# A recurrence step's small matmuls put in one fixed order in TensorE's queue, and its preparation moved to ordinary rank

## The chip, the core and the metric

One core of one Trainium2 chip runs the whole kernel. The metric is the time of one execution on the device in microseconds (us). The kernel before took 2898.03 us, the median of three runs (2893.39, 2898.03 and 2906.78 us).

## The reference, cut to what matters

One layer of a hybrid backbone works on 1024 latent tokens and 256 context tokens, all in float32. A joint input projection feeds two groups of heads. The first is differential attention, 8 heads over 1792 keys. The second is an RWKV-7 recurrence with 16 heads of size 64 that is scanned in both directions; one step of it is

```
sa = einsum('bhvk,bhk->bhv', S, -kk_t)
S  = S * w_t[:, :, None, :] + sa[..., None] * b_t[:, :, None, :] + v_t[..., None] * k_t[:, :, None, :]
y  = einsum('bhvk,bhk->bhv', S, r_t)
```

The gated outputs of both groups go through one output projection, a residual add and a final norm. The kernel doesn't scan token by token: it takes 32 tokens (a chunk) at once, so that a step of the recurrence becomes a few small matrix products.

## The kernel before, in words

**The stages.** The kernel first normalizes the tokens and makes the modulation. Then comes the long stage of input projections (lines 336 to 338), which also prepares, for each pair of heads, the recurrence's operands: the line-451 products with their mask, the transposes of line 455, and spills to DRAM. The third stage, `mix_phase`, holds the recurrence, the attention, the norm of the recurrence's outputs and the output projection. A tail finishes the attention's last blocks and the last part of the projection.

**The recurrence.** Heads are taken in two sets of eight (four pairs of heads, in two duos). A set has five segments of 256 tokens, first the context's and then four of the latents; a segment has eight chunks. That makes 80 steps, one for each chunk. Two steps in a row are a *part* (40 parts): the operands of a part are loaded together into one of two slots (tiles `L` and `R`, `load_part`, lines 774 to 784), and the inverses that its chunks need are loaded into one tile `Tb` (`load_inv`, line 795). All loads are issued on SP's queue.

**A step**, function `step`, in the order of its text:

- The *corrections*: 16 matmuls (line 907), each with a 96-row, 32-column stationary operand and 64 moving columns, in four column positions of the array (0, 32, 64, 96), into the left half of PSUM tile `bank[0]`. Four ScalarE copies (line 914) bring them into `R`. If the step is the last of its part, the first half of the next part's *preparation* follows (`prep(j + 1, 0, yb)`): 16 matmuls with 32 by 32 stationary operands (line 805) and four ScalarE copies into `L` (line 808).
- `fill(0)`: a share of the other work is emitted here: attention blocks by a running credit, the inverses, norms, and the projection.
- The *state group*: 16 matmuls (line 926) with 128-row, 64-column stationary operands in two column positions (0, 64), into `bank[1]`; then four VectorE multiplies by the decay (line 937), which write the next step's state into `R`.
- The *output group*: 16 matmuls (line 950), 128 rows by 32 columns, in four column positions, into the right half of `bank[0]`, and one ScalarE copy (line 952). In the last step of a part, the second half of the preparation (`prep(j + 1, 1, yb)`) follows.
- `fill(1)`: the rest of the step's share of other work.

Every float32 matmul stands in the trace as two passes, so a group of 16 matmuls counts x32. Both preparation halves use the one PSUM tile `yb`. The state group of part j + 1 reads what both halves wrote; its corrections read the loaded part of `L` alone.

**What sets the order.** Each engine works its queue in order. The queue's order is made at build time: a scheduler takes, among the instructions that it holds to be ready, the one with the lowest rank; the rank is the place in the text. `ahead(500)` (a high-priority block) ranks what stands in it 500 places earlier, and on leaving the block the count goes on from where it stood when the block was entered. So the state group's block and the output group's block, which follow one another, begin at the same rank. All three groups and both halves of the preparation stand in such blocks. `held(x)` makes the first matmul of a group wait, by semaphore, for all four copies or multiplies that came before it; the other fifteen have only the waits of their own operands.

Of the kernel before, what the change touches and what calls it, by code (L numbers as in the profile page):

```python
# [83 lines left out]
def tile_kernel(ctx: ExitStack, tc: tile.TileContext, i: dict, o: dict, heads=H, phases=3):  # L84
# [38 lines left out]
    with ExitStack() as p1:  # L123
# [373 lines left out]
        def b_k(p):  # L497
# [43 lines left out]
            if p == heads - 1:  # L541
                yield
                yield from b_inv()
                if phases >= 2:
                    pr.close()
                    mix.append(mix_phase(p2, tc, i, o, s, ident, nhalf, dram, td0, neglam, subg, lnh, heads, psm))
                    yield from mix[0]
# [195 lines left out]
def mix_phase(ctx, tc, i, o, s, ident, nhalf, dram, td0, neglam, subg, lnh, heads, psm):  # L743
    nc = tc.nc
# [7 lines left out]
    for w in duos:  # L752
        for n in range(2):
            L = cp.tile([P, 2, 2, 2, HN, P], F32, name=f"L{w}{n}")
            R = cp.tile([P, HN, 2, 2, P], F32, name=f"R{w}{n}")
# [42 lines left out]
    def prep(j, w, pp):  # L798
        L = slots[w, j % 2][0]
        Tb = Tbs[j][:, 2 * w:2 * w + 2]  # L800
        for e in range(2):
            for c in range(HN):
                for q in range(4):
                    n = 96 * (HN * e + c)
                    nc.tensor.matmul(pp[32 * q:32 * q + 32, n:n + 96], Tb[96:128, e, HN * q + c, :],  # L805
                                     L[96:128, e, q // 2, q % 2, c, 0:96], start=True, stop=True, tile_position=(96, 32 * q))
        for q in range(4):
            nc.scalar.copy(L[96:128, :, q // 2, q % 2, :, 0:96],  # L808
                           pp[32 * q:32 * q + 32, 0:192 * HN].rearrange("p (e c y) -> p e c y", e=2, y=96))
# [28 lines left out]
    bank = [psx.tile([P, 512], F32, name=f"bank{n}") for n in range(2)]  # L838
    yb = psx.tile([P, 512], F32, name="yb")
# [41 lines left out]
    def ahead(n):  # L881
        return tc.high_priority(offset=n) if n else nullcontext()
# [3 lines left out]
    def hold(x):  # L886
        whole.append(x.ins.name)

    def held(x):
        for y in whole:  # L890
            tc.add_manual_dep(x.ins, y, mybir.DependencyInfo(mybir.DependencyClass.Sync, mybir.DependencyReason.DATA))
        whole.clear()

    def step(j, k, fill):
        m, f = j // NF, j % NF
        c = HN * f + k
        p0, sg = items[m]
        hv = lambda h: slice(64 * h, 64 * h + 64)
        later_prep = k == HN - 1 and j + 1 < n_part
        with ahead(HPC):  # L900
            for d in range(2):
                for e in range(2):
                    for w in duos:
                        L, R = slots[w, j % 2]
                        for h in range(2):
                            u, o_ = 64 * w + 32 * h, 128 * d + 64 * e
                            x = nc.tensor.matmul(bank[0][u:u + 32, o_:o_ + 64], L[0:96, e, h, d, k, 96:128],  # L907
                                                 R[0:96, k, d, e, hv(h)], start=True, stop=True, tile_position=(0, u))
                            held(x)
            for w in duos:  # L910
                R = slots[w, j % 2][1]
                for h in range(2):
                    u = 64 * w + 32 * h
                    hold(nc.scalar.copy(R[96:128, k, :, :, hv(h)],  # L914
                                        bank[0][u:u + 32, 0:256].rearrange("p (d e v) -> p d e v", d=2, e=2)))
            if later_prep:
                prep(j + 1, 0, yb)
        fill(0)
        with ahead(HPC):
            for w in duos:  # L920
                L, R = slots[w, j % 2]
                for e in range(2):
                    for d in range(2):
                        for h in range(2):
                            o_ = 256 * w + 128 * d + 64 * e
                            x = nc.tensor.matmul(bank[1][hv(h), o_:o_ + 64], L[:, e, h, d, k, 0:64],  # L926
                                                 R[:, k, d, e, hv(h)], start=True, stop=True, tile_position=(0, 64 * h))
                            held(x)
            for w in duos:
                if k < HN - 1:  # L930
                    dst = slots[w, j % 2][1][0:64, k + 1]
                elif f == NF - 1 and sg == 3:
                    continue
                else:
                    dst = slots[w, (j + 1) % 2][1][0:64, 0]
                for h in range(2):
                    hold(nc.vector.tensor_tensor(dst[:, :, :, hv(h)], bank[1][hv(h), 256 * w:256 * w + 256].rearrange("p (d e v) -> p d e v", e=2, d=2),  # L937
                                                 wcs[p0][hv(h), 2 * w:2 * w + 2, sg + 1, :, c:c + 1].rearrange("p e d o -> p d e o").broadcast_to([HD, 2, 2, HD]), op=ALU.mult))
        g = c // HN
        if k == 0:  # L940
            ysb[m, g] = cp.tile([P, HN, NL, HD], F32, tag="ys", name=f"ys{m}_{g}", bufs=YBUF)
        with ahead(HPY):
            for w in duos:
                L, R = slots[w, j % 2]
                for e in range(2):
                    o_ = 256 + P * w + 64 * e
                    for h in range(2):
                        for d in range(2):
                            q = 64 * d + 32 * h
                            nc.tensor.matmul(bank[0][q:q + 32, o_:o_ + 64], L[:, e, h, d, k, 64:96], R[:, k, d, e, hv(h)],  # L950
                                             start=True, stop=True, tile_position=(0, q))
            nc.scalar.copy(ysb[m, g][:, k], bank[0][:, 256:512].rearrange("p (x v) -> p x v", x=NL))  # L952
            if later_prep:
                prep(j + 1, 1, yb)
        fill(1)

    def store_y(m, g):
        p0, sg = items[m]
        y = ysb.pop((m, g))
        for d in range(2):  # L960
            t0 = tok0(sg, d)
            for h in range(2):
                q = 64 * d + 32 * h
                dst = s["y"][p0 // NL, t0:t0 + SEG, d, h].rearrange("(c t) w v -> t c (w v)", t=CH)
                dst = (dst[:, ::-1] if d else dst)[:, HN * g:HN * g + HN]
                nc.sync.dma_start(dst, y[q:q + 32].rearrange("t c x v -> t c (x v)"))
# [449 lines left out]
    def turn(q, k=0):  # L1416
        if len(q) > k and next(q[k], "end") == "end":
            q.pop(k)
# [10 lines left out]
    def fill(pos):  # L1429
        for _ in range(2):  # L1430
            state["credit"] += total / (4 * n_tick) * RATES[2 * state["t"] // n_tick]
            while state["credit"] > 0 and state["n"] < heads * NT - NT + 6:
                r = next(att, None)
                if r is None:
                    break
                turn(outs)
                state["credit"] -= r
            while state["ninv"] < 33 * (state["t"] + INVA + _ / 4 + pos / 2) / NC:
                next(state["inv"], None)
                state["ninv"] += 1  # L1440
            turn(norms)
            turn(norms, 1)
            turn(projs)
# [8 lines left out]
    for t in range(n_tick):  # L1452
        m, c = t // NC, t % NC
        p0, sg = items[m]
        j, k = t // HN, t % HN
        state["t"] = t
        for f in later.pop(t, []):
            f()
        if c == 0:
            for w in duos:  # L1460
                start_item(w, m)
            if sg == 2 and m + 2 < n_item:
                load_pairs(m + 2)
        if 1 <= j and j + 1 < n_part:
            if k == 0:
                load_part(j + 1)
        step(j, k, fill)
        if k == HN - 1:
            at(t + 1, lambda m=m, g=c // HN: store_y(m, g))
        if c < NC - 1:  # L1470
            continue
        for sg_, gs in ((-1, (8,)), (2, (2, 4)), (3, (0, 6))):
            if sg == sg_:
                for g0 in gs:
                    for w in duos:
                        at(t + 3, lambda p=p0 + 2 * w, g0=g0: norms.append(norm(p, g0)))
        if sg == (3 if m < 5 else 0):
            for w in duos:
                at(t + 1, lambda j=p0 // 2 + w: projs.append(project(j)))
# [97 lines left out]
```

## Time and profile before

| | us |
|---|---|
| median of three runs | 2898.03 |
| profiled execution, its own time | 2893.28 |
| its span, first to last instruction | 2891.3 |
| TensorE busy in the span | 2751.5 |
| VectorE busy | 1477.8 |
| ScalarE busy | 1224.6 |
| GpSimd busy | 1130.1 |

The profile's engines are PE (TensorE's matmuls), PEld (its weight loads, beside PE), DVE (VectorE), ACT (ScalarE), POOL (GpSimd) and SP (SyncE, which only issues DMAs here). Idle time of an engine counts only where the others wait for it. The recurrence's loop stands between 1242 us (its first correction starts at 1242.61 us) and 2612 us (its last state product starts at 2610.89 us); what comes before is the projections' stage, and what comes after is the tail.

### The profile page before, as it was taken

How to read it: one execution, taken by the hardware profiler on the slowest of the kernel's cores; microseconds unless marked ns; L12 is line 12 of the kernel's file. 1: busy time of each engine (PE TensorE's matmuls, PEld its weight loads, DVE VectorE, ACT ScalarE, POOL GpSimd, SP SyncE). 2: the span in 40 equal slices, each digit the busy share in tenths (PEclk: the TensorE clock that was granted, in tenths of full speed). 3: DMA queues.
4: the chain of work that ended last, by engine and by line, in shares of the span. 5: the costliest groups of instructions: out<-in, count | busy, mean ns of one | idle time of the engine just before them, and what ended most of it. 6: DMA issues, size and time to landing. Idle time of an engine off the chain costs nothing.

```text
span 2891.3 us, 60416 instructions
## 1 busy us (share of the span) xinstructions
PE 2751.5 (95%) x23907; PEld 2156.8 (75%) x23907; DVE 1477.8 (51%) x2950; ACT 1224.6 (42%) x2528; POOL 1130.1 (39%) x1665
## 2 busy tenths in 40 slices
PE   6999999999999999889999999999999999998886
PEld 5888888888788887767667767776777777776675
DVE  5655656464555554324544445454643343445667
ACT  3333434333333433224545445554544454444343
POOL 4243432434333334733552533561662110105365
PEclk9999999999999999968999989999999999999898
DMA  7466655566556556695676655747566578548534
GB/s 232 102 156 165 172 150 152 153 168 155 140 141 158 145 154 157 159 209 125 138 147 121 140 111 109 155 89 177 134 148 172 139 169 175 138 108 234 169 124 164
DMA packets 518010, 437.55 MB, mean 151 GB/s; under 512 B 157831, under 2 KB 462131, under 8 KB 512608
## 3 DMA queue, kind: packets, MB, share of 16 engines
q1 hardware_dynamic: 515632, 427.94, 59.3%
q0 software_dynamic: 2096, 5.75, 1.1%
q8 instruction: 189, 3.10, 0.5%
q14 instruction: 93, 0.76, 0.1%
HBM read 258.69 MB, written 163.86 MB: 146 GB/s over the span
## 4 chain that ended last, share of the span: by engine, by line
PE 75%; DMA 7%; DVE 6%; POOL 5%; SPq 3%; ACT 3%; issue 2%; POOLq 0%; DVEq 0%; ACTq 0%
PE bank L926 12%; PE bank L950 10%; PE sc L1069 6%; PE po L1114 5%; PE pa L1099 3%; PE pg L451 3%; PE yb L805 2%; PE pso L1322 2%; PE pso L1324 2%; PE pso L1323 2%; PE bank L907 1%; PE ptk L455 1%; PE psg_v L338 1%; PE psg_v L336 1%; PE psg_v L337 1%
## 5 line engine op out<-in xcount | busy, mean ns | idle before, releaser
L926 PE MATMUL bank<-R,L 128*64 128x64 f32 x2560 | 429.3, 250 | 6.7 <-ACT R L914 5.9
L950 PE MATMUL bank<-R,L 128*32 128x64 f32 x2560 | 390.0, 235 | 0.0
L926 PEld LDWEIGHTS bank<-R,L 128*64 128x64 f32 x2560 | 250.2, 138 | 146.5 <-issue 20.8
L937 DVE TENSOR_TENSOR R<-bank,wc 64x256 f32<-64x256 f32 x312 | 131.5, 421 | 432.1 <-PE bank L926 419.5
L1069 PE MATMUL sc<-ka,q 128*128 128x512 f32 (+1 forms) x832 | 285.4, 435 | 18.9 <-DVE pb L1072 18.0
L1072 DVE TENSOR_SCALAR_CACHE_REDUCE pb<-sc,mn 128x512 f32<-128x512 f32 x256 | 191.5, 748 | 142.3 <-PE sc L1069 135.0
L1077 ACT ACTIVATE pb<-pb,mn 128x1536 f32<-128x1536 f32 (+1 forms) x160 | 218.2, 1364 | 80.3 <-DVE pb L1072 76.3
L950 PEld LDWEIGHTS bank<-R,L 128*32 128x32 f32 x2560 | 178.4, 109 | 92.8 <-issue 4.3
L952 ACT COPY ys<-bank 128x256 f32<-128x256 f32 x80 | 29.8, 372 | 464.6 <-PE bank L950 444.0
L1114 PE MATMUL po<-vk,aT 128*128 128x128 f32 x1600 | 223.4, 282 | 1.0 <-ACT aT L1101 1.0
L1114 PEld LDWEIGHTS po<-vk,aT 128*128 128x128 f32 x1600 | 206.2, 195 | 15.4 <-ACT aT L1101 1.8
L736 POOL TENSOR_TENSOR tmp<-aw,tt 128x31 f32<-128x31 f32 (+15 forms) x310 | 163.4, 527 | 126.2 <-DMA y<-ys 35.5
L481 POOL TENSOR_SCALAR ta<-ta,ka 128x256 f32<-128x256 f32 x80 | 85.6, 1070 | 294.1 <-DVE bk L479 293.9
L458 ACT COPY km<-ptk 64x256 f32<-64x256 f32 x320 | 117.4, 367 | 188.3 <-PE ptk L455 160.4
L738 POOL TENSOR_TENSOR tt<-tt,tmp 128x31 f32<-128x31 f32 (+15 forms) x310 | 181.1, 584 | 20.3
L1069 PEld LDWEIGHTS sc<-ka,q 128*128 128x128 f32 x832 | 136.9, 195 | 53.5 <-DVE pb L1072 30.4
L1091 DVE SCALAR_TENSOR_TENSOR pb<-pb,cc,pb 128x512 f32<-128x512 f32 (+1 forms) x208 | 165.2, 841 | 2.0
L808 ACT COPY L<-yb 32x384 f32<-32x384 f32 x312 | 146.3, 469 | 33.5 <-PE yb L805 29.1
L1101 ACT COPY aT<-pa 128x512 f32<-128x512 f32 (+1 forms) x208 | 115.1, 569 | 80.7 <-PE pa L1099 78.5
L452 DVE TENSOR_TENSOR km<-pg,msk 128x512 f32<-128x512 f32 x80 | 55.1, 688 | 179.7 <-PE pg L451 159.1
L1306 POOL TENSOR_TENSOR olo<-of,ohi 128x512 fp32r<-128x512 f32 x30 | 38.9, 1296 | 266.5 <-ACT ohi L1305 216.3
L1072 DVE TENSOR_SCALAR_CACHE_REDUCE pb<-sc 128x512 f32<-128x512 f32 (+1 forms) x160 | 101.2, 635 | 81.2 <-PE sc L1069 76.5
(354 smaller groups left out, 6555.2 us busy)
## 6 DMA issues: line engine op xcount, KB each, us to landing
kt<-km SPq DMA_DIRECT2D x160, 256.0 KB
L<-kt SPq DMA_DIRECT2D x80, 512.0 KB
acc<-acc SPq DMA_DIRECT2D x50, 512.0 KB
ra<-ra SPq DMA_DIRECT2D x160, 128.0 KB
L<-ra SPq DMA_DIRECT2D x80, 256.0 KB
R<-vb SPq DMA_DIRECT2D x160, 64.0 KB
y<-ys SPq DMA_DIRECT2D x160, 64.0 KB
yn<-y SPq DMA_DIRECT2D x40, 256.0 KB
```

The source lines that it names most:

```text
L458: nc.scalar.copy(km[64 * h:64 * h + 64, e:NC:2, 0:HD], pt[64 * e:64 * e + 64, :, 64 * h:64 * h + 64])
L736: e.tensor_tensor(mv, aw[:n, t, t + 1:CH].unsqueeze(2).broadcast_to([n, w, j]), tt[:n, t:t + 1, 0:j].broadcast_to([n, w, j]), op=ALU.mult)
L738: e.tensor_tensor(tt[:n, t + 1:CH, 0:j], tt[:n, t + 1:CH, 0:j], mv, op=ALU.add)
L808: nc.scalar.copy(L[96:128, :, q // 2, q % 2, :, 0:96], pp[32 * q:32 * q + 32, 0:192 * HN].rearrange("p (e c y) -> p e c y", e=2, y=96))
L926: x = nc.tensor.matmul(bank[1][hv(h), o_:o_ + 64], L[:, e, h, d, k, 0:64], R[:, k, d, e, hv(h)], start=True, stop=True, tile_position=(0, ...
L937: hold(nc.vector.tensor_tensor(dst[:, :, :, hv(h)], bank[1][hv(h), 256 * w:256 * w + 256].rearrange("p (d e v) -> p d e v", e=2, d=2), wcs ...
L950: nc.tensor.matmul(bank[0][q:q + 32, o_:o_ + 64], L[:, e, h, d, k, 64:96], R[:, k, d, e, hv(h)], start=True, stop=True, tile_position=(0, q))
L1069: nc.tensor.matmul(sc, q[:, v, m, qc], ka[:, m, 0:kn], start=(v == 0), stop=(v == 1))
L1072: nc.vector.tensor_scalar(pm[:, c * 512:c * 512 + kn], sc, -0.125, mn[:, c - 1:c] if c else None, op0=ALU.mult, op1=ALU.min, accum_out=mn[ ...
L1077: soon.append(lambda: nc.scalar.activation(v, v, AF.Exp, bias=mn[:, c:c + 1], scale=-1.0, accum_out=B["l"][:, m, B["b"]:B["b"] + 1]))
L1091: nc.vector.scalar_tensor_tensor(a, B["p"][1][:, v], B["cc"], a, op0=ALU.mult, op1=ALU.add)
L1114: nc.tensor.matmul(po, B["aT"][c][:, t * P:(t + 1) * P], vk[:, t, :], start=(c == 0 and t == 0), stop=(c == last and t == nt - 1))
```

## The change

Three things are changed in `step`. Each correction matmul is given an order-only dependency on the correction before it: it may not stand ahead of it in PE's queue, and no semaphore is added. The sixteen state matmuls are chained in the same way, and the sixteen output matmuls after them in the same chain, so the first output matmul stands behind the last state matmul. Both halves of the preparation leave the high-priority blocks: they are emitted after `fill(0)` and after `fill(1)`, at their ordinary place in the text. No operation is added or removed.

```
-    def held(x):
+    def held(x, chain):
         for y in whole:
             tc.add_manual_dep(x.ins, y, mybir.DependencyInfo(mybir.DependencyClass.Sync, mybir.DependencyReason.DATA))
         whole.clear()
+        if chain:
+            tc.add_manual_dep(x.ins, chain[-1], mybir.DependencyInfo(mybir.DependencyClass.NoSync, mybir.DependencyReason.SCHED_ONLY))
+        chain.append(x.ins.name)
...
         later_prep = k == HN - 1 and j + 1 < n_part
+        chain = []
         with ahead(HPC):
...
-                            held(x)
+                            held(x, chain)
...
-            if later_prep:
-                prep(j + 1, 0, yb)
         fill(0)
+        if later_prep:
+            prep(j + 1, 0, yb)
+        chain = []
         with ahead(HPC):
...
-                            held(x)
+                            held(x, chain)
...
-                            nc.tensor.matmul(bank[0][q:q + 32, o_:o_ + 64], L[:, e, h, d, k, 64:96], R[:, k, d, e, hv(h)],
-                                             start=True, stop=True, tile_position=(0, q))
+                            x = nc.tensor.matmul(bank[0][q:q + 32, o_:o_ + 64], L[:, e, h, d, k, 64:96], R[:, k, d, e, hv(h)],
+                                                 start=True, stop=True, tile_position=(0, q))
+                            if chain:
+                                tc.add_manual_dep(x.ins, chain[-1], mybir.DependencyInfo(mybir.DependencyClass.NoSync, mybir.DependencyReason.SCHED_ONLY))
+                            chain.append(x.ins.name)
             nc.scalar.copy(ysb[m, g][:, k], bank[0][:, 256:512].rearrange("p (x v) -> p x v", x=NL))
-            if later_prep:
-                prep(j + 1, 1, yb)
         fill(1)
+        if later_prep:
+            prep(j + 1, 1, yb)
```

## Rows read from the trace of the kernel before

**Rows 1.** The profile's page: the span, each engine's busy time with its share and its instructions, and the chain of work that ended last, by engine and by line.

```profile
span 2891.3 us, 60416 instructions
...
PE 2751.5 (95%) x23907; PEld 2156.8 (75%) x23907; DVE 1477.8 (51%) x2950; ACT 1224.6 (42%) x2528; POOL 1130.1 (39%) x1665
...
PE 75%; DMA 7%; DVE 6%; POOL 5%; SPq 3%; ACT 3%; issue 2%; POOLq 0%; DVEq 0%; ACTq 0%
PE bank L926 12%; PE bank L950 10%; PE sc L1069 6%; PE po L1114 5%; PE pa L1099 3%; PE pg L451 3%; PE yb L805 2%; PE pso L1322 2%; PE pso L1324 2%; PE pso L1323 2%; PE bank L907 1%; PE ptk L455 1%; PE psg_v L338 1%; PE psg_v L336 1%; PE psg_v L337 1%
```

**Rows 2.** Busy time of each engine in the recurrence's loop and in the tail: the stretch, its length, busy us and instructions of each engine, then the granted share of TensorE's clock, the mean busy share of the 16 DMA engines, and GB/s.

```profile
1242.00:2612.00 1370.00, 1346.47 (x13480) 981.84 (x13479) 614.83 (x1491) 652.93 (x1425) 495.62 (x907) 0.97 0.63 142
2612.00:2891.00 279.00, 224.36 (x1119) 178.05 (x1117) 191.57 (x407) 110.86 (x229) 137.17 (x175) 0.91 0.55 172
```

**Rows 3.** Timeline of PE alone, one step in the middle of the loop: start us, length us, line, operation, operands, shapes, number of passes merged. The two lines of the state and output groups go on alternating between the rows shown.

```profile
1527.02 0.65 PE L907 MATMUL bank<-R,L 96*32 96x64 f32 x32
1527.61 0.86 PE L805 MATMUL yb<-L,Tb 32*32 32x96 f32 x32
1528.40 1.21 PE L1069 MATMUL sc<-ka,q 128*128 128x512 f32 x4
1529.45 1.50 PE L1114 MATMUL po<-vk,aT 128*128 128x128 f32 x12
1530.88 0.33 PE L926 MATMUL bank<-R,L 128*64 128x64 f32 x2
1531.14 0.30 PE L950 MATMUL bank<-R,L 128*32 128x64 f32 x2
1531.37 0.33 PE L926 MATMUL bank<-R,L 128*64 128x64 f32 x2
...
1538.19 0.33 PE L926 MATMUL bank<-R,L 128*64 128x64 f32 x2
1538.45 0.30 PE L950 MATMUL bank<-R,L 128*32 128x64 f32 x2
1538.68 1.19 PE L1069 MATMUL sc<-ka,q 128*128 128x512 f32 x4
```

**Rows 4.** Groups of instructions by line over the whole span: line, engine, operation, operands, count, then busy us and mean ns of one, then idle time of the engine just before them and what ended it.

```profile
L926 PE MATMUL bank<-R,L 128*64 128x64 f32 x2560 | 429.3, 250 | 6.7 <-ACT R L914 5.9
L950 PE MATMUL bank<-R,L 128*32 128x64 f32 x2560 | 390.0, 235 | 0.0
L1077 ACT ACTIVATE pb<-pb,mn 128x1536 f32<-128x1536 f32 (+1 forms) x160 | 218.2, 1364 | 80.3 <-DVE pb L1072 76.3 <-DVE m L995 2.5
L808 ACT COPY L<-yb 32x384 f32<-32x384 f32 x312 | 146.3, 469 | 33.5 <-PE yb L805 29.1 <-DMA q<-qhi 0.4
L937 DVE TENSOR_TENSOR R<-bank,wc 64x256 f32<-64x256 f32 x312 | 131.5, 421 | 432.1 <-PE bank L926 419.5 <-POOL tmp L736 9.5
L914 ACT COPY R<-bank 32x256 f32<-32x256 f32 x320 | 115.9, 362 | 36.2 <-PE bank L907 32.0
```

**Rows 5.** Timeline of PE alone, two places in the loop where a few corrections stand between other matmuls; columns as in the timeline above.

```profile
1711.05 0.30 PE L907 MATMUL bank<-R,L 96*32 96x64 f32 x2
1711.28 0.50 PE L1069 MATMUL sc<-ka,q 128*128 128x512 f32 x1
...
1753.33 0.32 PE L907 MATMUL bank<-R,L 96*32 96x64 f32 x8
1753.58 0.66 PE L1099 MATMUL pa<-ident,pb 128*128 128x128 f32 x4
```

**Rows 6.** Timeline of PE alone: one whole group of line-451 products in the projections' stage (64-column stationary operands in two column positions, 64 moving columns), and what starts after it.

```profile
608.78 1.15 PE L451 MATMUL pg<-ra,bk 64*64 64x64 f32 x32 [0.62 <-POOL bk L483]
609.86 0.66 PE L455 MATMUL ptk<-ident,bk 128*128 128x128 f32 x4
```

**Rows 7.** Timeline of PE alone: 16 passes of full-size matmuls of the attention in the loop, and what starts after them.

```profile
1545.43 1.95 PE L1114 MATMUL po<-vk,aT 128*128 128x128 f32 x16
1547.14 0.71 PE L1069 MATMUL sc<-ka,q 128*128 128x512 f32 x2
```

**Rows 8.** The loop in stretches of some 69 us; the two with the highest DMA share in which PE never waits, columns as in the stretches above.

```profile
2132.00:2201.00 69.00, 69.00 (x737) 52.59 (x736) 29.28 (x73) 32.53 (x77) 31.95 (x54) 1.00 0.89 218
2406.00:2475.00 69.00, 69.00 (x699) 52.63 (x697) 21.84 (x53) 29.55 (x73) 7.89 (x15) 1.00 0.89 191
```

**Rows 9.** What SP's queue waited for in the loop: line and what it waited for, us in total, times, the longest.

```profile
SPq L783 <- PE bank L950: 168.5, 25, 24.6
SPq L795 <- PE yb L805: 87.8, 18, 21.8
SPq L966 <- ACT ys L952: 82.7, 20, 14.1
SPq L774 <- PE bank L950: 56.7, 20, 4.1
```

**Rows 10.** DMA issues of a part's loads: operands, queue, number over the whole kernel, KB each.

```profile
L<-kt SPq DMA_DIRECT2D x80, 512.0 KB
...
L<-ra SPq DMA_DIRECT2D x80, 256.0 KB
R<-vb SPq DMA_DIRECT2D x160, 64.0 KB
...
Tb<-td SPq DMA_DIRECT2D x40, 128.0 KB
```

## The prediction

> **What bounds the kernel now.** I read the page first. PE is busy 95% of the span, and the chain of work that ended last runs three quarters of its length through PE; its two largest lines are the state group (L926, 12%) and the output group (L950, 10%), together 22% of 2891 us, some 636 us [rows 1]. Then I cut the span at the recurrence's loop: in its 1370 us PE is busy 1346 us, or 98%, while DVE has 45%, ACT 48%, and the DMA engines 63% [rows 2]. So the loop is bound by PE's queue, and time taken out of PE there comes out of the loop until something else is full.
>
> The third view, PE's timeline of one step, shows what to look for: sixteen state matmuls and sixteen output matmuls stand strictly one by one, L926 and L950 in turn, and take from 1530.88 to 1538.68, 7.80 us. In the same step sixteen corrections, standing together, take from 1527.02 to 1527.61, 0.59 us [rows 3]. The matmuls are of like size. The mean of one pass is 250 ns (L926), which for a matmul of 64 columns is nearly all latency [rows 4]. The price of standing alone shows again where corrections are cut apart: two passes between other matmuls hold PE for 0.23 us (1711.05 to 1711.28), and eight passes, one round of the four column positions, hold it for 0.25 us [rows 5]. What costs is therefore the change from one shape of tile to another, about 0.2 us each time, and not the product.
>
> **The change, part by part.**
>
> *State and output group.* Two blocks of equal rank explain the strict turn; the chain ends it. Before, each turn of the shapes costs 0.26 us (1530.88 to 1531.14) and 0.23 us (1531.14 to 1531.37) [rows 3], so 16 x 0.49 = 7.84 us a step and 80 x 7.84 = 627 us in all, which agrees with the 636 us of the chain. After, no state group is seen whole in this trace. The nearest row is the L451 group: as many passes, 64 stationary columns in two positions, 64 moving columns, 1.08 us from its start to the next line's [rows 6]. The output group has the corrections' four positions and columns, and 128 rows in place of 96, so I take their 0.59 us [rows 3]. That makes 1.67 us a step, 134 us in 80 steps: 627 - 134 = 493 us come off PE.
>
> The bounds: the state group can't be cheaper than the corrections' 0.59 us, which is 39 us more gained. At worst positions don't overlap at all, and each pass costs what a full-size one does, 1.71 / 16 = 0.107 us [rows 7]: both groups then take 32 x 0.107 = 3.42 us, and of the 493 us only 80 x (7.84 - 6.84) = 80 us are left. The L451 and correction rows overlap positions, and the shapes are theirs, so I take 493.
>
> Against this stands a rule of the Trainium skill (TensorE: Matmul & The Clock Gate, part 3, The mechanism): a weight load overlaps running matmuls only where the row group differs. All state matmuls use the same rows, so by it the sum would be nearer the 80 us than the 493. The corrections also share their rows, and their 0.59 / 32 = 18 ns a pass [rows 3] contradict it for column positions.
>
> *Corrections.* They stand whole already in the step shown [rows 3]; the chain fixes their mutual order and keeps no other matmul out. I count 0. The fifteen others now queue behind the first, which waits for all four multiplies; at most three multiplies, 3 x 0.421 = 1.26 us [rows 4], are lost to the recurrence's own chain, and PE has attention to do meanwhile. No semaphore is added.
>
> *Preparation.* The same 39 x 2 halves, each 0.79 us on PE (1527.61 to 1528.40) [rows 3] and 4 x 0.469 = 1.88 us on ACT [rows 4], only later: they now queue behind attention that is older in the text, on PE and on ACT. They issue no DMA. Who waits is the next part's state group, and `Tb`, which is free for SP's next load only after them (87.8 us of waits already [rows 9]). More cuts in the groups would cost some 0.24 us each; three in each of 78 halves would be 56 us, none is 0. I take 0, since no more attention is about than before, and keep 56 for the range.
>
> *What is late next.* PE alone would leave 1370 - 493 = 877 us of loop. In that time ACT would be at 653 / 877 = 74% and DVE at 70%, but the DMA engines hold 0.63 x 1370 = 863 us of work [rows 2], 98% of it. They can't run full: they load into buffers that the recurrence must first release, which is where SP's queue waits now (168.5 + 56.7 us on the output products, 82.7 us on `ys`) [rows 9], and all later loads queue behind such a wait. What this code sustains without holding PE up is a share of 0.89, in two stretches of 69 us [rows 8]. For the whole loop I take a little less, 0.87: 863 / 0.87 = 992 us. The bounds are 877 us (PE alone) and, if the DMA engines' idle 507 us shrink only as PE's work does (877 / 1370), 863 + 325 = 1188 us. 992 is nearer the first because a queue with transfers waiting in it wastes less than one without.
>
> One more unknown is the clock: 0.97 granted in the loop, 0.91 in the tail, where PE is 80% busy [rows 2]. If the loop fell to that, PE's 854 us (1346 - 493) would grow by 6%, some 50 us; in a loop that DMA bounds I count 0 and keep it for the range.
>
> **The sum.** 1242 us before the loop are untouched, then 992, then the tail's 279 us [rows 2], and 2 us outside the span: 2515 us, against the profiled execution's own 2893.28 us. That execution stands 5 us under the median of the runs, well within their spread, so I add nothing: **2515 us**, a gain of 13%.
>
> **The rivals.**
>
> *PE alone decides.* DMA's idle time closes as fast as PE asks. For it: two stretches at 0.89 with PE never idle. Against: 98% on average is not 0.89. It gives 1242 + 877 + 279 + 2 = 2400 us, up to 2440.
>
> *The recurrence's own chain becomes the bound.* With preparation at ordinary rank the state group of a new part loses its lead. A step's chain is 0.59 + 4 x 0.362 + 1.08 + 4 x 0.421 = 4.8 us, two steps 9.6, the preparation in series 2 x (0.79 + 1.88) = 5.3: 14.9 us a part. There are 12 handovers from engine to engine, each behind whatever runs there, up to 1.4 us on ACT (L1077) or 1.7 us on PE [rows 4, 7]; at 1 us each it is 27 us a part, 1080 us in 40 parts, 2603 us; at 1.3 us each, 2750 us. Against: a part has 877 / 40 = 22 us of PE work in any case, and preparation needs nothing of the part before it but its `Tb`.
>
> *Slower: loads fall into the chain.* A slot is free for part j + 1 only after the last output product of part j - 1. A part loads 2 x 512 + 2 x 256 + 4 x 64 + 128 = 1920 KB [rows 10], 13.5 us at the loop's 142 GB/s [rows 2]. If late preparation keeps the loads from running beside the part before, a part takes 27 + 13.5 = 40.5 us, the loop 1620 us, the whole 3143 us. It turns slower than before from 1370 / 40 = 34.3 us a part. Against it: two slots, and no more bytes than now.
>
> *The chain doesn't do it.* Passes keep the full-size price, or older attention matmuls come between so often that the shapes turn as before. With the 80 us above the time is 1242 + 1290 + 279 + 2 = 2813 us; with nothing gained, 2893 us. By the skill's rule on weight loads it is the first of these; the corrections' row [rows 3] speaks against that one, and that the same row stands whole among attention matmuls against the other.
>
> **How the numbers follow.** The likeliest case (groups whole, DMA and PE together the bound, 2440 to 2620 us) has a chance of 0.66; PE alone 0.13; the recurrence's chain (2600 to 2760) 0.13; the chain of order without effect 0.04, half of it near 2813 and half at no change; loads in the chain 0.04. The range is 2420 to 2680 us: it takes in the bounds of the clock and of cut preparation (2515 + 50 + 56 = 2621), and leaves out the ends of PE alone and of the recurrence's chain, and the last two cases. Faster by over 0.5% (about what a measurement of this kernel can tell from no change) is 0.94, within it 0.02, slower 0.04.
>
> **What would show it.** Right: in PE's timeline one L926 x32 of about 1.1 us, then one L950 x32 of about 0.6 us, in most steps; both lines' share of the chain gone from 22% to about 5%; a loop of about 990 us with the DMA share near 0.87 and PE below 90%. DMA is the bound if PE's and SP's waits name loads (`L`, `Tb`, `ka`); the recurrence's chain is, if PE idles before L926 for ACT's L808 or L914. Wrong at the root: L926 groups whole and still near 3.4 us, or L926 and L950 in short pieces. Wrong in size: a DMA share above 0.93, or under 0.8 with PE waiting for ACT or DVE.

## The result and the profile after

The changed kernel takes 2570.57 us, the median of four runs (2558.65 to 2573.49), against 2902.41 us, the median of four runs of the kernel before: a ratio of 0.8846, with a 95% interval from 0.8799 to 0.8892. The profiled execution took 2572.84 us.

In the changed file the lines lie a little lower: the corrections are line 911, their copies 918, the state group 931, the multiplies 942, the output group 955, the attention's matmuls 1077, 1107 and 1122. The page, as in [rows 1]:

```profile
span 2570.8 us, 60369 instructions
...
PE 2320.6 (90%) x23907; PEld 1891.8 (74%) x23907; DVE 1480.2 (58%) x2950; ACT 1221.3 (48%) x2528; POOL 1138.7 (44%) x1665
...
PE 51%; DMA 18%; POOL 10%; DVE 7%; SPq 5%; issue 5%; ACT 4%; POOLq 0%; DVEq 0%; ACTq 0%
PE sc L1077 4%; PE po L1122 3%; DMA L<-kt 3%; PE pg L451 3%; POOL tt L738 2%; PE bank L931 2%; POOL tmp L736 2%; PE pa L1107 2%; PE yb L805 2%; DMA yn<-y 2%; PE pso L1330 2%; DMA acc<-acc 2%; PE pso L1332 2%; PE pso L1331 2%; PE ptk L455 1%
```

PE's count of instructions is the same, its busy time 431 us shorter. The state group has gone from 12% of the chain to 2%, the output group out of its list; in their place stand DMAs (7% to 18%) and many small things. No single line bounds the kernel any more.

PE's timeline of one step, as in [rows 3]:

```profile
1756.90 0.73 PE L1077 MATMUL sc<-ka,q 128*128 128x256 f32 x4
1757.62 1.15 PE L931 MATMUL bank<-R,L 128*64 128x64 f32 x32
1758.70 0.65 PE L955 MATMUL bank<-R,L 128*32 128x64 f32 x32
1759.28 0.66 PE L1107 MATMUL pa<-ident,pb 128*128 128x128 f32 x4
```

The state group holds PE from 1757.62 to 1758.70, 1.08 us, the output group from there to 1759.28, 0.58 us: 1.66 us in place of 7.80. The output group stands whole, like this, in all 80 steps; the state group does in 59, and in the others further matmuls, mostly the attention's, still stand between its products. The two groups by line, as in [rows 4]; their mean pass still lasts some 235 ns, but passes now run beside each other:

```profile
L931 PE MATMUL bank<-R,L 128*64 128x64 f32 x2560 | 112.5, 237 | 14.7 <-ACT R L918 13.3 <-ACT L L808 1.0 <-issue 0.2
L955 PE MATMUL bank<-R,L 128*32 128x64 f32 x2560 | 56.5, 233 | 0.0
```

The loop (now from 1244 to 2315 us) and the tail, as in [rows 2]:

```profile
1244.00:2315.00 1071.00, 942.48 (x13622) 739.12 (x13622) 641.59 (x1548) 667.03 (x1457) 520.75 (x932) 0.91 0.84 185
2315.00:2571.00 256.00, 199.44 (x986) 157.25 (x974) 164.84 (x350) 93.23 (x198) 119.28 (x151) 0.89 0.52 170
```

The loop is 299 us shorter and the tail 23 us. PE, idle for 24 us of the loop before, is idle for 129 us now, and its granted clock has fallen from 0.97 to 0.91. What PE waits for in the loop (line, what it waited for, us, times, longest):

```profile
PE yb L805 <- DMA Tb<-td: 26.9, 8, 10.5
PE yb L805 <- DMA L<-kt: 16.9, 5, 4.4
PE sc L1077 <- DVE pb L1080: 14.4, 14, 3.7
PE bank L931 <- ACT R L918: 13.3, 13, 2.0
```

The first two are the preparation, waiting for the part's loads. What such a wait costs shows in PE's timeline around 1400 us, and in the busy times of the three stretches about it (the share after the engines' times is the granted clock):

```profile
1394.20 0.72 PE L1077 MATMUL sc<-ka,q 128*128 128x512 f32 x2
1399.31 0.60 PE L805 MATMUL yb<-L,Tb 32*32 32x96 f32 x12 [4.39 <-DMA L<-kt]
1399.83 0.69 PE L1107 MATMUL pa<-ident,pb 128*128 128x128 f32 x2
1400.45 1.98 PE L931 MATMUL bank<-R,L 128*64 128x64 f32 x32
1402.36 0.95 PE L955 MATMUL bank<-R,L 128*32 128x64 f32 x32
1403.24 0.71 PE L1122 MATMUL po<-vk,aT 128*128 128x128 f32 x4
```

```profile
1393.00:1400.00 7.00, 2.61 (x28) 1.95 (x28) 2.33 (x9) 2.85 (x10) 6.43 (x20) 0.97 0.97 214
1400.00:1403.00 3.00, 3.00 (x59) 2.55 (x63) 0.51 (x2) 0.37 (x1) 2.77 (x4) 0.50 1.28 189
1403.00:1416.00 13.00, 10.88 (x227) 8.15 (x218) 9.64 (x27) 11.19 (x25) 4.83 (x10) 1.00 0.99 213
```

PE waits 4.39 us for `L<-kt`; then the clock stands at 0.50, the lower of its two levels (1.2 GHz), and the state group takes 1.91 us in place of 1.08, until 0.50 gives way to 1.00 again. Such a wait is paid twice. Not every wait is: PE waits some 90 times in this loop, 38 times for over 1 us, and the trace has 24 stretches at half clock, 198 us together (92 us in the loop before). Each of the 24 begins within a few us after a wait.

### The profile page after: what moved, and what is told of

Read it like the earlier page. It is cut to its first block, busy times and chain, and to the rows that moved or that the text cites. A ratio compares the mean times of both kernels' runs of the same rounds, so it can differ in the third digit from the quotient of the medians.

```text
span 2570.8 us, 60369 instructions
## 1 busy us (share of the span) xinstructions
PE 2320.6 (90%) x23907; PEld 1891.8 (74%) x23907; DVE 1480.2 (58%) x2950; ACT 1221.3 (48%) x2528; POOL 1138.7 (44%) x1665
## 4 chain that ended last, share of the span: by engine, by line
PE 51%; DMA 18%; POOL 10%; DVE 7%; SPq 5%; issue 5%; ACT 4%; POOLq 0%; DVEq 0%; ACTq 0%
PE sc L1077 4%; PE po L1122 3%; DMA L<-kt 3%; PE pg L451 3%; POOL tt L738 2%; PE bank L931 2%; POOL tmp L736 2%; PE pa L1107 2%; PE yb L805 2%; DMA yn<-y 2%; PE pso L1330 2%; DMA acc<-acc 2%; PE pso L1332 2%; PE pso L1331 2%; PE ptk L455 1%
## 5 line engine op out<-in xcount | busy, mean ns | idle before, releaser
L1077 PE MATMUL sc<-ka,q 128*128 128x512 f32 (+1 forms) x832 | 294.8, 448 | 33.6 <-DVE pb L1080 26.3
L1122 PEld LDWEIGHTS po<-vk,aT 128*128 128x128 f32 x1600 | 212.5, 200 | 20.5 <-ACT aT L1109 6.2
L1099 DVE SCALAR_TENSOR_TENSOR pb<-pb,cc,pb 128x512 f32<-128x512 f32 (+1 forms) x208 | 165.0, 840 | 2.0
L805 PE MATMUL yb<-L,Tb 32*32 32x96 f32 x2496 | 107.5, 263 | 53.0 <-DMA Tb<-td 26.9
L1107 PE MATMUL pa<-ident,pb 128*128 128x128 f32 x800 | 132.7, 293 | 24.4 <-DVE acc L1324 19.1
L805 PEld LDWEIGHTS yb<-L,Tb 32*32 32x32 f32 x2496 | 64.7, 111 | 102.7 <-issue 59.5
L918 ACT COPY R<-bank 32x256 f32<-32x256 f32 x320 | 115.9, 362 | 47.8 <-PE bank L911 43.6
L1107 PEld LDWEIGHTS pa<-ident,pb 128*128 128x128 f32 x800 | 97.3, 149 | 49.1 <-DVE acc L1324 22.1
```

The costliest lines, as they stand in the source:

```text
L1077: nc.tensor.matmul(sc, q[:, v, m, qc], ka[:, m, 0:kn], start=(v == 0), stop=(v == 1))
L1099: nc.vector.scalar_tensor_tensor(a, B["p"][1][:, v], B["cc"], a, op0=ALU.mult, op1=ALU.add)
L1107: nc.tensor.transpose(pt[:, t * P:(t + 1) * P], B["p"][0][:, 512 * c + t * P:512 * c + (t + 1) * P], ident)
L1122: nc.tensor.matmul(po, B["aT"][c][:, t * P:(t + 1) * P], vk[:, t, :], start=(c == 0 and t == 0), stop=(c == last and t == nt - 1))
```

## The experiments

All times are medians; each ratio is to runs of the kernel before on the same chip. The groups of runs were on different chips, so between groups the ratios are compared.

**The parts of the change, one at a time.** The first run (e1) keeps the chains and puts the preparation back where it was:

```
+            if later_prep:
+                prep(j + 1, 0, yb)      # inside ahead(HPC), before fill(0)
         fill(0)
-        if later_prep:
-            prep(j + 1, 0, yb)
...                                      # and prep(j + 1, 1, yb) inside ahead(HPY)
```

> The chains of the change, with both halves of the preparation put back into the high-priority blocks. Theory A (the whole gain is the end of the turns between two shapes of tile): groups of 1.08 and 0.59 us, PE's work in the loop as in the changed kernel, time 2540 to 2610 us against its 2570. Rival B (the ordinary rank of the preparation is part of the gain, because it lets attention through): slower than the changed kernel by over 50 us, 2620 or more.

It took 2626.15 us, ratio 0.9037 (0.9005 to 0.9070): slower than the changed kernel's 0.8846, with intervals apart. The chains alone give most of the gain, 278 of 332 us; theory A's claim to all of it fell by its own bound. The loop and tail, and PE's longest waits:

```profile
1245.00:2323.00 1078.00, 942.45 (x13316) 726.53 (x13319) 607.24 (x1454) 637.25 (x1400) 494.82 (x898) 0.88 0.81 175
2323.00:2632.00 309.00, 253.68 (x1292) 201.96 (x1280) 204.01 (x443) 123.97 (x254) 146.20 (x183) 0.90 0.55 172
```

```profile
PE yb L805 <- DMA L<-kt: 37.6, 11, 9.1
PE yb L805 <- DMA Tb<-td: 28.2, 7, 10.7
```

The loop is as long as the changed kernel's, but 306 fewer of PE's instructions are done in it; they come in the tail, 53 us longer. So the ordinary rank does two things: less waiting for loads at the preparation (66 us here, 44 there in these two rows), and more attention inside the loop. Over all waits PE's idle time differs by only 7 us (136 and 129), so the second weighs more. Two more things help to explain why the same busy time of PE holds more work there: the clock (0.88 here, 0.91 there), and fewer cuts. PE's order changes from one tile shape to another 963 times in this loop and 799 times in the changed kernel's; the corrections stand whole in 57 steps here and in 77 there. How the 55 us divide among them was not tried.

The second run (e2) is the other half alone: the kernel before with the two `prep` calls moved out of their blocks as in the change, and no chain.

> The preparation at ordinary rank alone, no chain: state and output products go on in turn. Theory A: 2890 to 2930 us, no gain, at most 20 us lost to preparation groups cut in more pieces. Rival B: 2800 us or less.

2919.05 us, ratio 1.0055 (1.0025 to 1.0084), as theory A had it. Its loop and tail:

```profile
1246.00:2666.00 1420.00, 1392.75 (x13623) 1010.65 (x13619) 649.84 (x1559) 671.88 (x1460) 517.40 (x939) 0.95 0.65 142
2666.00:2918.00 252.00, 200.86 (x970) 159.48 (x968) 161.42 (x338) 91.66 (x194) 115.48 (x143) 0.89 0.48 159
```

It shifts the same attention into the loop (13623 instructions, against 13480 in [rows 2]), but that loop is full of PE work and pays more for them than the tail gives back (50 us longer, with the clock at 0.95 against 0.97; the tail is 27 us shorter). The same edit costs 15 us where PE is the bound and gives some 55 us once it isn't.

**Another way to end the turns (e3).** The kernel before with one number changed:

```
-HPY = 500
+HPY = 480
```

> The kernel before with one number changed: the output group's block is ranked 480 places ahead in place of 500, so its products rank just behind the state group's four multiplies. No chain, preparation as before. Theory A (the turns come from equal ranks, and ending them by any means gives the gain): state groups near 1.08 us in most steps, time 2550 to 2630 us. Rival (only an explicit chain keeps products together): state and output products still in turn, 2850 us or more.

2675.39 us, ratio 0.9213 (0.9178 to 0.9248). The turns do come from the equal ranks: with a rank 20 places lower, state and output products stand in turn no more. The size was missed by 45 us. The run to compare it with is the one with the chains alone, since both keep the preparation in its block: 2675 us against 2626. Its loop:

```profile
1239.00:2381.00 1142.00, 1015.83 (x13353) 752.84 (x13353) 609.77 (x1462) 642.75 (x1405) 496.02 (x899) 0.86 0.77 166
```

PE's timeline shows what a rank leaves open: attention matmuls still come between. The output group is whole in 51 steps (72 with the chains alone), and PE's order changes shape 1193 times in the loop (963 there, 3101 in the kernel before).

```profile
1706.21 1.50 PE L805 MATMUL yb<-L,Tb 32*32 32x96 f32 x30 [6.33 <-DMA L<-kt]
1707.64 1.11 PE L926 MATMUL bank<-R,L 128*64 128x64 f32 x14
1708.68 1.22 PE L1069 MATMUL sc<-ka,q 128*128 128x512 f32 x2
1709.71 1.05 PE L1114 MATMUL po<-vk,aT 128*128 128x128 f32 x4
1710.69 0.70 PE L926 MATMUL bank<-R,L 128*64 128x64 f32 x8
```

**How much a turn costs (e4).** The changed kernel with another order in its chain, two state and two output products in turn (the output products move into the state group's block):

```
                 for e in range(2):
-                    for d in range(2):
+                    for n in range(2):
                         for h in range(2):
...                          # state products (w, e, d=n, h)
+                        for d in range(2):
+                            # output products (w, e, h=n, d), held(x, chain)
```

> The changed kernel with the order of its chain altered: two state products, two output products, and so on, eight rounds a step; the same products, sixteen turns of shape a step in place of two (and thirty-two before). Theory A (a turn costs about 0.25 us, the products next to nothing): 8 x (0.26 + 0.235) = 3.96 us a step, 2.3 us more than in the changed kernel, 183 us more of PE's work; since the loop has some 129 us of idle PE time, part of it is hidden: 2640 to 2750 us. Rival (the product's own time is what was hidden by grouping): a time near the kernel before's, 2850 or more; or near the changed kernel's, under 2600, if turns are not the cost.

2648.08 us, ratio 0.9139 (0.9097 to 0.9181), within theory A's bounds. A stretch of its timeline, and its loop:

```profile
1699.83 0.34 PE L931 MATMUL bank<-R,L 128*64 128x64 f32 x4
1700.10 0.31 PE L937 MATMUL bank<-R,L 128*32 128x64 f32 x4
1700.33 0.34 PE L931 MATMUL bank<-R,L 128*64 128x64 f32 x4
```

```profile
1246.00:2385.00 1139.00, 1088.23 (x13622) 815.95 (x13622) 651.32 (x1551) 671.27 (x1457) 516.84 (x931) 0.94 0.78 175
```

Two products take 0.27 and 0.23 us where one took 0.26 and 0.23 [rows 3]: a piece of one shape has its price, however few products stand in it. Half the pieces cost half: 4.0 us a step. PE's work in the loop is 146 us above the changed kernel's, the time only 78 us, since the loop's idle PE time shrank to 51 us: a part of what grouping saves is handed back as waiting.

This run alone doesn't tell the turn from the overlap of column positions, since the two products of a piece stand in two positions. The starts of single passes in the kernel before tell them apart: the second pass of a lone state product starts 0.107 us after its first, and the next shape 0.152 us after that; for a lone output product it is 0.080 and 0.149 us. So of the 0.26 and 0.23 us some 0.15 are the turn, and the rest are the product's own two passes, which run one behind the other and which a product in another position can share (passes of one shape in different positions start 0.007 us apart). It isn't the change of PSUM tile that costs: among the attention's 128 by 128 matmuls the next pass starts 0.112 us later whether it writes the same PSUM tile (L1114 after L1114) or another (L1099 after L1114). The Trainium skill (TensorEngine Tiling (Array Packing), Tiling Modes, Key Properties) says that a change of tiling mode drains the engine; the 0.15 us at each turn between 128x64 and 128x32 agree.

**What bounds the loop now: bytes, or their place?** Three runs take bytes off the DMA engines and keep the number of issues (`ka` has three buffers in them, in place of four). Left out is the attention of heads 1 to 7 on their own data:

```
+        if h:
+            dm = ap.tile([P, 2, 8], F32, tag="dmk", name=f"dmk_{h}_{g}", bufs=2)
+            ...                      # the same DMAs, 8 columns each
+            ks[h, g] = ks[0, g]
+            return
         ka = ap.tile(...)            # Q and V alike
```

On the changed kernel (e5):

> The changed kernel with bytes taken off the DMA engines: from the second attention head on, each load of Q, K and V fetches 8 columns into a scratch tile in place of the whole block, and the products read the first head's blocks. The number of DMA issues stays; some 37 MB of the loop's 198 MB go. Left out: the attention of heads 1 to 7 on their own data. Theory L (the part loads land late because the DMA engines are near full, and PE's waits and its half clock follow from that): the 53 us of PE waiting at the preparation fall under 20 us, less time at half clock, 2480 to 2530 us against 2570. Rival Q (the bytes don't matter, the loads are late because of their place in SP's queue and the release of the slots): 2550 us or more.

On the kernel with the chains alone (e6):

> The same bytes taken off the kernel that has the chains but keeps the preparation in the high-priority blocks. Theory L (the ordinary rank helps only by putting the preparation behind other work while late loads land): with loads on time the two places of the preparation are worth the same, so it ends within 20 us of the run before it, 2490 to 2545 us, a gain of some 100 us on its own 2626. Rival (the place of the preparation matters for another reason, such as the recurrence's own chain or the attention's): it stays 40 us or more above the run before it.

On the kernel before (e9):

> The same bytes taken off the kernel before. Both theories: PE alone bounds it, so 2875 to 2915 us, within 1% of the kernel before. If it gains over 30 us, loads cost the kernel before as well, and the bytes are not a sign of the changed kernel's new bound.

They took 2531.07 us (ratio 0.8728, 0.8695 to 0.8761), 2598.48 us (0.8975, 0.8936 to 0.9014) and 2881.89 us (0.9931, 0.9907 to 0.9955). The loop of the first, and its waits at the preparation:

```profile
1241.00:2268.00 1027.00, 922.35 (x13611) 725.85 (x13599) 646.97 (x1548) 667.21 (x1457) 517.65 (x932) 0.92 0.72 159
```

```profile
PE yb L805 <- DMA Tb<-td: 34.1, 10, 10.5
PE yb L805 <- DMA L<-kt: 5.9, 2, 3.1
```

Theory L fell in the main, and rival Q's claim that bytes don't matter fell too. The first run lies 1 us above theory L's range and 19 us under rival Q's. But the waits are theory L's mechanism, and they stayed: 40 us in these rows, where it asked for under 20. The DMA share went from 0.84 to 0.72, and the loop got only 44 us shorter, with 105 us of PE idle. Nor did the two places of the preparation come together: 67 us lie between the first two runs, no less than the 55 with all bytes. Bytes count for a part, 34 us by the ratios (40 by the medians), against the 20 us (18) that the kernel before gains. (The expectation's 37 MB of "198 MB" is the changed loop's traffic, 185 GB/s x 1071 us.)

Next (e7), the 160 small loads of the inverses (144 of them in the loop) were moved from SP's queue to GpSimd's:

```
-            nc.sync.dma_start(aw[u:u + 4 * HN], kt[:, :, 96:128])
+            nc.gpsimd.dma_start(aw[u:u + 4 * HN], kt[:, :, 96:128])
```

> The changed kernel with the 16 small loads of each inverse (144 issues in the loop, 82 us of SP's issuing time, 4.6 MB) issued on GpSimd's queue. Rival Q (SP's queue delays the part loads): 2510 to 2550 us. Theory L (bytes and engine time of the DMA engines, which stay the same): 2555 to 2585 us.

2585.91 us, ratio 0.8921 (0.8896 to 0.8946): no gain, a little slower, 1 us above theory L's range. Its waits at the preparation:

```profile
PE yb L805 <- DMA Tb<-td: 60.9, 14, 12.2
PE yb L805 <- DMA L<-kt: 6.0, 3, 5.5
```

The wait for `L<-kt` fell from 16.9 to 6.0 us, as rival Q would have it, and the wait for `Tb` rose from 26.9 to 60.9. GpSimd computes the inverses that `Tb` is loaded from, and with the issues on its queue it is busy for 607 us of the loop in place of 521; that the inverses came later for this reason is likely, but not shown. So the run shows that this move gains nothing. Whether SP's issuing time delays the part's other loads stays open.

**The preparation's place, and its one buffer.** Two runs (e8a, e8b) hold the preparation back by order-only dependencies on products of the recurrence, `behind` in:

```
+                    if behind:
+                        tc.add_manual_dep(x.ins, behind, ...NoSync, SCHED_ONLY...)
...
-            prep(j + 1, 0, yb)
+            prep(j + 1, 0, yb, chain[-1])   # e8a: last correction; e8b passes the last output of the step before
...
-            prep(j + 1, 1, yb)
+            prep(j + 1, 1, yb, chain[-1])   # e8a: last output; e8b passes the last correction
```

> The changed kernel, with the preparation held to its place in the text by order-only dependencies: the first half behind the last correction of its own step, the second half behind the step's last output product. No byte and no operation changes. Theory M (PE waits at the preparation because its place in PE's queue comes sooner than its loads land, the single Tb above all, and every such wait costs half clock afterwards): the 53 us of waiting at L805 fall under 15, half clock from 198 us to under 150, time 2490 to 2545 us. Rival R (the recurrence's own chain is what is left, so that a later preparation delays it): waits move to the state group for the preparation's copies, 2570 us or more.

> As the run before it, with both halves half a step sooner: the first behind the last output product of the step before, the second behind the last correction of its step. Theory M: loads have one step of some 12 us to land, more than the 4 to 9 us from issue to landing, so the waits at L805 still go, and the copies stand off the recurrence's chain: 2490 to 2545 us, no slower than the run before it. Rival R: 20 us or more faster than the run before it, as the chain is shorter by the second half and its copies.

2553.96 us, ratio 0.8805 (0.8769 to 0.8841), and 2557.49 us, 0.8825 (0.8771 to 0.8879): the first is the fastest of the kernels here that leave nothing out, 12 us under the changed kernel by the ratios, though the intervals overlap. Both missed theory M's 2490 to 2545, and rival R's 2570 for the first and its 20 us for the second didn't come either. The first one's loop, and its longest wait at the preparation:

```profile
1246.00:2295.00 1049.00, 916.50 (x13630) 729.25 (x13629) 646.10 (x1547) 668.03 (x1459) 519.73 (x932) 0.92 0.86 189
```

```profile
PE yb L805 <- DMA Tb<-td: 26.1, 7, 10.2
```

The wait for `L<-kt` is gone from L805, though with 5 us each for `L<-ra` and for ScalarE's copies some 36 us of waits are left there, where theory M asked for under 15; in the second run it is 43 us for `Tb` alone. PE's idle time isn't gone, 132 us, nor the half clock, 178 us where theory M asked for under 150. The last two runs take `Tb`'s reloads away as well, from the changed kernel (e10) and from e8a (e11):

```
+        if j:
+            Tbs[j] = Tbs[0]
+            return
         Tb = cp.tile(...)
```

> The changed kernel without the loads of Tb after the first part: all parts use the first part's inverses, which stay in place. Left out: 39 loads of 128 KB, the wait for the one buffer, and with them the right values of the recurrence. Theory S (the single Tb, refilled only after both halves of the part before, is what PE waits for at the preparation): the waits at L805 fall from 53 us to under 25, half clock under 160 us, 2520 to 2550 us. Rival (all waits are a pool: take one away and the next in the part's chain takes its place): 2555 to 2575 us.

> The kernel with the preparation held to its place in the text, and without the loads of Tb after the first part (the same left out). Theory S: with both causes of waiting at L805 gone, 2500 to 2535 us, PE's idle time in the loop under 100 us against 132. Rival: 2540 to 2560 us.

2571.93 us, ratio 0.8861 (0.8833 to 0.8889), and 2542.87 us, 0.8780 (0.8753 to 0.8807): the rivals' bounds both times. The longest wait at the preparation (line 808 in these files) of the first, then that of the second with the largest of all its waits, and the second's loop:

```profile
PE yb L808 <- DMA L<-kt: 42.5, 15, 9.0
```

```profile
PE pxo L1170 <- POOL ob L1164: 21.6, 4, 9.3
...
PE yb L808 <- DMA L<-kt: 15.1, 4, 8.3
```

```profile
1244.00:2289.00 1045.00, 915.26 (x13620) 725.44 (x13609) 649.89 (x1552) 669.91 (x1461) 525.40 (x932) 0.92 0.84 185
```

With `Tb` out of the way, `L<-kt` takes its waits over, 42.5 us where the two had 43.8, and the time stands still. With both eased PE is idle for 130 us all the same, at other handovers, the largest of them a wait for GpSimd. Theory S fell: what is left is no single wait.

## Why the prediction was right, and where its sizes were off

**State and output group: right to the row.** 1.08 and 0.59 us were taken from the L451 group and the corrections; 1.08 and 0.58 us were measured. One of the two rows carried less than the prediction asked of it. The L451 products are 64 by 64 tiles (`pg[hs]` from `bk[hs]`, [rows 6]): the two heads differ in their rows as well as in their columns, while all state products share their rows. Only the corrections' row spoke for overlap at shared rows. That both kinds of group take 1.08 us is what the run shows; the prediction had no row for it, and in this it was lucky. Its price of a turn, some 0.2 us, holds 0.15 us of turn and the lone product's own passes; the sum used the whole piece and is not touched by that. Busy time of all `bank` matmuls and then of the preparation's, in the loop before:

```profile
1242.00:2612.00 1370.00, 717.06 (x7744) 477.51 (x7744) 131.46 (x312) 150.72 (x416) 0.97 0.63 142
...
1242.00:2612.00 1370.00, 88.31 (x2496) 58.44 (x2496) 0.97 0.63 142
```

and after:

```profile
1244.00:2315.00 1071.00, 230.44 (x7744) 187.58 (x7744) 131.11 (x312) 150.12 (x415) 0.91 0.84 185
...
1244.00:2315.00 1071.00, 107.54 (x2496) 64.66 (x2496) 0.91 0.84 185
```

717 - 230 = 487 us, against 493 in the sum. By the weight-load rule of the Trainium skill that was weighed there, the gain would have been nearer 80 us; for column positions at shared rows the measurement decides against it.

**The sum by stages.** 1242 + 992 + 279 were forecast, 1244 + 1071 + 256 measured: the loop came out 79 us longer, the tail 23 us shorter, and the total 55 us above 2515 (58 us for the profiled execution), within the likeliest case's 2440 to 2620 us. In the sum's own terms, 863 / 0.87 became 900 / 0.84: the DMA engines' busy time was not the fixed amount that the term supposed.

**Mis-sized: PE's work in the loop.** It was to be 854 us and is 942. The preparation accounts for 19 us (88.3 to 107.5), inside the 0 to 56 kept for it; I had taken 0. All other matmuls went from 1346 - 717 - 88 = 541 us to 942 - 230 - 108 = 604 us. About 25 of those 63 us came over from the tail (224 to 199 us of PE work), a shift that the prediction lacked. The rest, near 38 us, fits the clock (198 us at half clock in the loop, 92 before), but no run sets it apart: 0.91 is the very value that I named as a bound, priced at 50 us, and counted as 0 on the ground that DMA would hide it. How much of it the loop's time paid is not shown; in e4, 146 us more of PE work cost 78.

**The next bound: near the mark, for a wrong reason.** The forecast of 0.87 of DMA share and 992 us looks close to 0.84 and 1071, and its signs came (PE below 90%, loads named in its waits). But the argument was throughput, and e5 speaks against it as the main cause: with 0.12 less of DMA share, 739 us of DMA work in place of 900, the loop got 44 us shorter. So it is luck that the loop's time came out near. SP's waits on the output products did shrink (225 us in [rows 9], 47.5 us after). What the runs show in its place is a pool of short waits, some 129 us, that replace one another (e10, e11), with stretches at half clock behind a part of them. The reading that fits is that loads and copies land later than their users' places in PE's queue suppose; why the scheduler's order supposes them sooner was not tried, so the cause of what is left stays open.

**The preparation: wrong in sign.** I treated its ordinary rank as harmless or as a danger. Given the chains it gives about 55 us (e1); without them it costs 15 (e2). The step that failed was to price a move only by what it delays, and not by what it lets through: 306 more of PE's instructions in a loop of the same length.

**The rivals.** PE alone (2400 us) and the loads in series (3143 us) didn't come. The recurrence's own chain is a part of the pool (13.3 us for L918), not the bound. That the chain doesn't hold was refuted by the groups, the state group whole in 59 of 80 steps and the output group in all.

## What to carry to other kernels

Look in PE's timeline for short matmuls of different tile shape in turn: their price is the turn, with the lone product's own passes, and a whole group of the same shape elsewhere in the trace tells what they will cost together (see that its row and column positions are the same, too). Give such groups an order of their own; with ranks alone other matmuls still come between. Once PE is no longer full, allow for the half clock that follows some of its waits, and expect the next handover to take over when one wait is removed.

## What was not expected of the hardware

Two passes or four of a tile shape between other shapes hold PE equally long (0.26 and 0.27 us for the state products, 0.23 us each for the output products). A single wait of 4.39 us left the granted clock at 0.50 and stretched the next group from 1.08 to 1.91 us. And the DMA share can read over 1: 1.28 in the 3 us from 1400, so a share of 0.98 worked out ahead, as the prediction's 863 of 877 us, is not by itself a bound. Where the bound lies no run shows; the highest share over a whole loop here was 0.87 (e7).
